# Forget attention of a four-layer block: scores as float32r products over all 128 rows, mask last

## Chip, cores and metric

The kernel runs on one core of one Trainium2 chip. The metric is the device time of one execution in microseconds (us). Three runs of the kernel before gave 1043.25, 1047.08 and 1048.91 us; their median is 1047.08.

## What is computed

The input is a sequence of 256 tokens of 1024 numbers. Two layers of a first block (a gated recurrence and a sparse attention), then an even layer, a feed-forward layer, an odd layer and another feed-forward layer run one after the other, all in float32. The change touches the odd layer alone, and in it the forget attention: eight heads of 64 numbers, causal, with a sum of log forget gates added to the logits.

```python
def forgetting_attention(q, k, v, f_logit, b_f):
    ...
    q, k, v = heads(q), heads(k), heads(v)
    log_f = jax.nn.log_sigmoid(f_logit.astype(jnp.float32) + b_f.astype(jnp.float32))
    c = jnp.cumsum(log_f, axis=1).transpose(0, 2, 1)
    ...
        logits = (jnp.einsum('bhqd,bhkd->bhqk', qb, k).astype(jnp.float32) * scale
                  + cb[..., None] - c[:, :, None, :])
        q_pos = start + jnp.arange(Q_BLOCK)
        logits = jnp.where(key_pos[None, :] <= q_pos[:, None], logits, -jnp.inf)
        p = jax.nn.softmax(logits, axis=-1)
        return jnp.einsum('bhqk,bhkd->bhqd', p.astype(v.dtype), v)
```

The term `cb` is the same for all keys of a query, so the softmax drops it.

## The kernel before

Every large product is made of float32r products in three parts: operands are split into a high part (rounded to float32r) and a low part (the rest, rounded too), and high x high, high x low and low x high are added up in PSUM (`mm3`, line 363). Weights come from HBM in pieces of 128x1024 numbers (512 KB): SP issues the load into `raw` (3 buffers), ScalarE writes the high part `whi`, VectorE the low part `wlo` (5 buffers each, `wload`, line 333). ScalarE and VectorE do this beside all their other work, in the order of one queue each, and so does SP with its loads. The order within each queue is set when the program is built, by a scheduler, and not by the order of the lines: products of a later step are put between those of an earlier one, where it expects a wait.

The odd layer (`odd_layer`, line 1139) projects v, the forget logits, q and k (`oq`, 8 groups of 24 products with 256 columns), then runs the attention in two halves of 128 queries (H = 0 with 128 keys, H = 1 with 256 keys), and beside it the projection of the gate `g` (`og`, 48 products of 512 columns, lines 1213 and 1214). Behind these come the gate's normalisation and mixing (`pm`, line 1224), the projection `u` (`ou`, line 1231), and the output projection.

q and k lie transposed, two heads in one group of 128 rows: head n has rows 0 to 63 if n is even and 64 to 127 if it is odd (`qT`, `kT`, lines 1178 to 1186, in float32). In `attention` (line 527) heads go by parity: for H = 0 four heads of one parity share a PSUM tile of 512 columns (`as`, two buffers), for H = 1 two heads. The tile begins with the mask for all 512 columns, a bf16 product with the identity. Then each head adds the forget sums (`extra`, line 1189: a float32r product of `cr`, which holds the sums in two parts, and `onehot`, which picks the head) and its q times k, in float32 over 64 rows:

```python
                mm(p3, identb, bm(causal[:, (1 - H) * P:], hb), True, False)
                for j in range(hb):
                    n = 2 * (j0 + j) + par
                    extra(p3[:, j, :], n, nk)
                    mm(p3[:, j, :], q(n), k(n)[:, :nk], False, j == hb - 1)
```

VectorE takes the maxima from PSUM (`anm`), ScalarE the exponentials with their sums (`pr`), VectorE scales them (`af`), TensorE transposes (`apt`), VectorE copies the transposes to SBUF (`pts`), and TensorE multiplies with v (`fo`).

Of the kernel before, what the change touches and what calls it, by code (L numbers as in the profile page):

```python
# [10 lines left out]
F32 = mybir.dt.float32  # L11
F32R = mybir.dt.float32r
BF = mybir.dt.bfloat16
U8 = mybir.dt.uint8
AF = mybir.ActivationFunctionType
OP = mybir.AluOpType
AX = mybir.AxisListType.X

P = 128
T = 256  # L20
# [200 lines left out]
def body(ctx: ExitStack, tc: tile.TileContext, a: dict, offs: dict, out: bass.AP):  # L221
# [4 lines left out]
    wk = ctx.enter_context(tc.tile_pool(name="wk", bufs=1))  # L226
# [5 lines left out]
    BUFS = dict(t2=2, lf=4, kT=3, vh=2, pr=2, pts=2, gate=4, s4=4, s1=2, w8=2, kk=1, y=2, nz=2,  # L232
                sm=4, sn=2, ss=4, sr=4, R=2, sh=3, sa=6, sc=6, sf=4,
                acc=3, pA=2, pM=1, pB=1, pC=1)
# [4 lines left out]
    def s2(name, dt=F32, tag="t2"):  # L239
        return wk.tile([P, 512], dt, tag=tag, name=name, bufs=BUFS[tag])  # L240

    def s4(name, dt=F32, tag="s4"):
        return wk.tile([P, 1024], dt, tag=tag, name=name, bufs=BUFS[tag])
# [10 lines left out]
    def dma(o, i):  # L254
        nc.sync.dma_start(o, i)
# [3 lines left out]
    def act(o, i, f, **kw):  # L259
        A.activation(o, i, f, **kw)  # L260

    def tt(o, x, y, op):
        V.tensor_tensor(o, x, y, op=op)  # L263
# [5 lines left out]
    def bm(ap, n):  # L269

        return ap.unsqueeze(1).to_broadcast([ap.shape[0], n, ap.shape[1]])
# [88 lines left out]
    def mm(o, l, r, start=True, stop=True):  # L360
        PE.matmul(o, l, r, start=start, stop=stop)  # L361
# [165 lines left out]
    def attention(H, q, k, pv, extra):  # L527

        nk = (H + 1) * P
        hb = 512 // nk
        sums = small("asum", 8, "sa")
        nm = small("anm", 8, "sa")
        for part in range(8 // (2 * hb)):
            pt2 = []
            for par in range(2):
                ps = ps_("as", "pA")
                p3 = ps.rearrange("p (h s) -> p h s", h=hb)
                j0 = part * hb  # L540
                mm(p3, identb, bm(causal[:, (1 - H) * P:], hb), True, False)
                for j in range(hb):
                    n = 2 * (j0 + j) + par
                    extra(p3[:, j, :], n, nk)
                    mm(p3[:, j, :], q(n), k(n)[:, :nk], False, j == hb - 1)
                c = slice(par * 4 + j0, par * 4 + j0 + hb)
                V.tensor_reduce(nm[:, c], p3, axis=AX, op=OP.max, negate=True)
                pr = s2("pr", tag="pr")
                pr3 = pr.rearrange("p (h s) -> p h s", h=hb)
                for j in range(hb):  # L550
                    i = par * 4 + j0 + j
                    act(pr3[:, j, :], p3[:, j, :], AF.Exp, bias=nm[:, i:i + 1], accum_out=sums[:, i:i + 1])
                f = small("af", 4, "sf")[:, :hb]
                V.reciprocal(f, sums[:, c])
                tt(pr3, pr3, bc(f, nk), OP.mult)
                pt = ps_("apt", ("pM", "pB")[par])
                for j in range(hb):
                    for b in range(H + 1):
                        i = b * hb + j
                        PE.transpose(pt[:, i * P:(i + 1) * P], pr3[:, j, b * P:(b + 1) * P], ident)  # L560
                pts = s2("pts", tag="pts")
                V.tensor_copy(pts, pt)
                pt2.append(pts)
            pv(j0, hb, pt2)
# [574 lines left out]
    def odd_layer(nx, nxt):  # L1139
# [35 lines left out]
        act(cr[:8], fe, AF.Copy)  # L1175
        tt(cr[32:40], fe, cr[:8], OP.subtract)

        qT = s4("oqT").rearrange("p (j t) -> p j t", j=4)
        kT = s4("okT").rearrange("p (j t) -> p j t", j=4)
        for nm, dst, sc in (("q", qT, 0.125), ("k", kT, 1.0)):  # L1180
            for j in range(0, 4, 2):
                ps = pacc("oq")
                for i in range(2):
                    proj_fm(ps[:, i * T:(i + 1) * T], x, win(f"{nm}{j + i}"))
                V.scalar_tensor_tensor(dst[:, j:j + 2, :], ps.rearrange("p (j t) -> p j t", j=2), sc, bm(R, 2),
                                       op0=OP.mult, op1=OP.mult)
        y = new_x("yE")

        def extra(s, n, nk):
# [2 lines left out]
        for H in range(2):  # L1192
            sl = slice(H * P, (H + 1) * P)
            po = ps_("fo", "pC")

            def pv(j0, hb, pts):
                for j in range(hb):
                    for b in range(H + 1):
                        for par in range(2):
                            n = 2 * (j0 + j) + par  # L1200
                            i = b * hb + j
                            mm(po[par * 64:(par + 1) * 64, (j0 + j) * P:(j0 + j + 1) * P], vs[b][:, n * 64:(n + 1) * 64],
                               pts[par][:, i * P:(i + 1) * P], b == 0, b == H)

            attention(H, lambda n: qT[(n % 2) * 64:(n % 2 + 1) * 64, n // 2, sl],
                      lambda n: kT[(n % 2) * 64:(n % 2 + 1) * 64, n // 2, :], pv, extra)
            split(y, slice(0, 4), sl, po.rearrange("p (j t) -> p j t", j=4))
        sb = s2("sgub", tag="y")
        sap = a["sgub"]
# [161 lines left out]
```

## Time and profile before

| | |
|---|---|
| median of three runs | 1047.08 us |
| the profiled execution | 1047.36 us, its span 1045.6 us |
| TensorE busy | 1020.2 us, 98% |
| its weight loads | 887.3 us, 85% |
| VectorE busy | 803.6 us, 77% |
| ScalarE busy | 593.5 us, 57% |
| GpSimd busy | 39.5 us, 4% |
| mean granted TensorE clock | 0.985 of full speed |
| HBM read | 164.36 MB, 158 GB/s over the span |

All times of rows count from the start of the span. PE is TensorE's products, PEld its weight loads, which run beside the products; DVE is VectorE, ACT ScalarE, POOL GpSimd, SP the engine that issues the loads. PEclk is the clock that was granted to TensorE, 1.00 being 2.4 GHz and 0.50 being 1.2 GHz. Products are pipelined and their ends are modelled, so the distance from one start to the next tells more than a duration.

### The profile page before, as it was taken

What the parts mean: (1) busy time and instruction counts of PE and PEld (TensorE: products, weight loads), DVE (VectorE), ACT (ScalarE), POOL (GpSimd) and SP (SyncE); (2) the same over time, 40 slices, a digit from 0 to 9 for tenths busy, and PEclk for the clock granted to TensorE, in tenths of its full rate; (3) what the DMA queues carried; (4) which work ended last, traced back from release to release, by engine and by line L of the source; (5) the groups of instructions that cost most, each with busy time, mean ns of one, the idle gap of its engine ahead of it and who ended that gap; (6) DMA issues with size and microseconds to landing.
All of it is one profiled execution on the core that took longest, in us unless ns stands there. A gap on an engine that the chain in (4) does not pass through costs nothing.

```text
span 1045.6 us, 17333 instructions
## 1 busy us (share of the span) xinstructions
PE 1020.2 (98%) x6604; PEld 887.3 (85%) x6604; DVE 803.6 (77%) x1508; ACT 593.5 (57%) x1049; POOL 39.5 (4%) x45
## 2 busy tenths in 40 slices
PE   7999999999999999999999999999999999999997
PEld 6778887778788776899889999998976889999996
DVE  5578888887788788778968877777644769777776
ACT  6654456567544564666657655556633557555553
POOL 1001100000002000000100000000000100000000
PEclk9999999999999999999999999999977999999999
DMA  8742643365523433655656666664631556666661
GB/s 300 242 145 55 217 130 90 93 222 157 185 69 108 137 101 92 184 161 174 208 160 188 198 186 193 184 183 132 213 109 51 165 147 201 186 188 192 184 182 60
DMA packets 47140, 166.54 MB, mean 159 GB/s; under 512 B 5456, under 2 KB 6480, under 8 KB 46416
## 3 DMA queue, kind: packets, MB, share of 16 engines
q1 hardware_dynamic: 47056, 165.43, 52.1%
q8 instruction: 52, 0.85, 0.3%
q14 instruction: 32, 0.26, 0.1%
HBM read 164.36 MB, written 1.05 MB: 158 GB/s over the span
## 4 chain that ended last, share of the span: by engine, by line
PE 78%; DVE 8%; ACT 5%; DMA 4%; issue 2%; POOL 2%; SPq 0%; POOLq 0%; ACTq 0%; DVEq 0%
PE up L361 24%; PE pd L361 11%; PE po L361 7%; PE as L361 3%; PE pg L361 3%; DVE wlo L263 3%; PE nz L361 2%; PE oq L361 2%; PE hgo L361 2%; DMA raw<-in_win_dram 2%; PE no L361 2%; PE pl L361 2%; POOL hr L408 2%; ACT whi L260 2%; PE Q L361 2%
## 5 line engine op out<-in xcount | busy, mean ns | idle before, releaser
L260 ACT ACTIVATE whi<-raw 128x1024 fp32r<-128x1024 f32 (+2 forms) x295 | 309.5, 1053 | 239.6 <-PE up L361 59.6
L263 DVE TENSOR_TENSOR wlo<-raw,whi 128x1024 fp32r<-128x1024 f32 (+2 forms) x295 | 357.1, 1213 | 93.5 <-ACT whi L260 90.8
L361 PE MATMUL pd<-whi,fhl 128*128 128x512 f32 x352 | 115.8, 391 | 0.0
L361 PE MATMUL up<-xFlo,whi 128*128 128x256 f32 x352 | 99.6, 283 | 0.5 <-DVE xFlo L432 0.5
L361 PE MATMUL up<-xDlo,whi 128*128 128x256 f32 x352 | 99.6, 283 | 0.5 <-DVE xDlo L432 0.5
L361 PE MATMUL up<-xDhi,whi 128*128 128x256 f32 x352 | 99.4, 283 | 0.2 <-ACT xDhi L260 0.2
L361 PE MATMUL up<-xFhi,whi 128*128 128x256 f32 x352 | 99.4, 283 | 0.2 <-ACT xFhi L260 0.2
L361 PE MATMUL up<-xFhi,wlo 128*128 128x256 f32 x352 | 99.5, 283 | 0.0
L361 PE MATMUL up<-xDhi,wlo 128*128 128x256 f32 x352 | 99.5, 283 | 0.0
L361 PEld LDWEIGHTS pd<-whi,fhl 128*128 128x128 f32 x352 | 66.2, 188 | 14.1 <-ACT fhl L260 0.9
L1027 DVE SCALAR_TENSOR_TENSOR fc<-fp,colp,fc 128x255 f32<-128x255 f32 (+1 forms) x176 | 73.5, 479 | 0.8 <-ACT fc L260 0.7
L361 PE MATMUL pd<-wlo,fhl 128*128 128x512 f32 x176 | 69.1, 392 | 0.0
L361 PEld LDWEIGHTS up<-xFlo,whi 128*128 128x128 f32 x352 | 67.5, 192 | 1.5 <-DVE xFlo L432 0.7
L361 PEld LDWEIGHTS up<-xDlo,whi 128*128 128x128 f32 x352 | 67.5, 192 | 1.5 <-DVE xDlo L432 0.7
L361 PEld LDWEIGHTS up<-xFhi,whi 128*128 128x128 f32 x352 | 67.3, 192 | 1.2 <-ACT xFhi L260 0.5
L361 PEld LDWEIGHTS up<-xDhi,whi 128*128 128x128 f32 x352 | 67.3, 192 | 1.2 <-ACT xDhi L260 0.5
L361 PEld LDWEIGHTS up<-xFhi,wlo 128*128 128x128 f32 x352 | 67.5, 192 | 0.0
L361 PEld LDWEIGHTS up<-xDhi,wlo 128*128 128x128 f32 x352 | 67.5, 192 | 0.0
L260 ACT ACTIVATE fc<-fp,colp 128x256 f32<-128x256 f32 x88 | 47.8, 589 | 2.7 <-DVE fp L263 2.6
L260 ACT ACTIVATE pr<-as,anm 128x128 f32<-128x128 f32 (+1 forms) x80 | 32.6, 423 | 27.9 <-PE apt L1011 9.6
L260 ACT ACTIVATE fhl<-fc 128x256 fp32r<-128x256 f32 x44 | 18.3, 415 | 44.9 <-DVE fc L263 44.9
L263 DVE TENSOR_TENSOR fp<-up,R 128x512 f32<-128x512 f32 x44 | 30.4, 691 | 15.8 <-PE up L361 15.8
(473 smaller groups left out, 2485.2 us busy)
## 6 DMA issues: line engine op xcount, KB each, us to landing
raw<-in_up_dram SPq DMA_DIRECT2D x88, 512.0 KB, 3.6
raw<-in_win_dram SPq DMA_DIRECT2D x64, 512.0 KB, 4.2
raw<-in_down_dram SPq DMA_DIRECT2D x44, 512.0 KB, 3.6
raw<-in_ein_dram SPq DMA_DIRECT2D x20, 512.0 KB, 4.1
raw<-in_oin_dram SPq DMA_DIRECT2D x20, 512.0 KB, 4.0
raw<-in_wout_dram SPq DMA_DIRECT2D x16, 512.0 KB, 3.6
raw<-in_wpg_dram SPq DMA_DIRECT2D x16, 512.0 KB, 4.2
cw<-in_cw_dram SPq DMA_DIRECT2D x4, 1024.0 KB, 5.3
```

What stands on the lines that cost most here:

```text
L260: A.activation(o, i, f, **kw)
L263: V.tensor_tensor(o, x, y, op=op)
L361: PE.matmul(o, l, r, start=start, stop=stop)
L408: G.tensor_tensor(o, v, mh[:, :v.shape[1]], op=OP.pow)
L1027: V.scalar_tensor_tensor(dst[:, k:], src[:, :T - k], w, dst[:, k:], op0=OP.mult, op1=OP.add)
```

## The change

The scores are made as three float32r products over all 128 rows. For each parity there is a tile of queries whose 64 own rows hold the high part and whose other 64 rows hold the low part of the same heads; the high part of the keys (`KA`) and their low part (`KB`) each stand twice, on both halves of the rows. So queries times `KA` is high x high plus low x high, and queries times `KB` is high x low plus low x low. ScalarE writes the high parts (8 copies of 64x512), VectorE the low parts (8 subtractions), and SP issues twelve copies of 64x512 from SBUF to SBUF that fill the other halves. The mask is the last product of a tile, and covers only the last 128 columns of each head.

```diff
@@ attention
-                mm(p3, identb, bm(causal[:, (1 - H) * P:], hb), True, False)
                 for j in range(hb):
                     n = 2 * (j0 + j) + par
+                    for i, kn in enumerate(k(n)):
+                        mm(p3[:, j, :], q(n), kn[:, :nk], j + i == 0, False)
                     extra(p3[:, j, :], n, nk)
-                    mm(p3[:, j, :], q(n), k(n)[:, :nk], False, j == hb - 1)
+                mm(p3[:, :, nk - P:], identb, bm(causal[:, P:], hb), False, True)
@@ odd_layer
-        qT = s4("oqT").rearrange("p (j t) -> p j t", j=4)
-        kT = s4("okT").rearrange("p (j t) -> p j t", j=4)
-        for nm, dst, sc in (("q", qT, 0.125), ("k", kT, 1.0)):
+        big = [wk.tile([P, 2, 4, T], F32R, tag="w8", name="oqk", bufs=BUFS["w8"]) for par in range(2)]
+        QA, KA = ([t[:, i] for t in big] for i in range(2))
+        KB = [wk.tile([P, 4, T], F32R, tag=n, name="okb", bufs=1) for n in ("kA", "kk")]
+        own = [slice(par * 64, (par + 1) * 64) for par in range(2)]
+        for nm, sc in (("q", 0.125), ("k", 1.0)):
             for j in range(0, 4, 2):
                 ps = pacc("oq")
                 for i in range(2):
                     proj_fm(ps[:, i * T:(i + 1) * T], x, win(f"{nm}{j + i}"))
-                V.scalar_tensor_tensor(dst[:, j:j + 2, :], ps.rearrange("p (j t) -> p j t", j=2), sc, bm(R, 2),
-                                       op0=OP.mult, op1=OP.mult)
+                t = s2("oqf", tag="t2").rearrange("p (j t) -> p j t", j=2)
+                V.scalar_tensor_tensor(t, ps.rearrange("p (j t) -> p j t", j=2), sc, bm(R, 2), op0=OP.mult, op1=OP.mult)
+                js = slice(j, j + 2)
+                lo = None if nm == "k" else s2("oql", F32R, "kT").rearrange("p (j t) -> p j t", j=2)
+                for par, o in enumerate(own):
+                    other = own[1 - par]
+                    hi = (QA if nm == "q" else KA)[par]
+                    act(hi[o, js], t[o], AF.Copy)
+                    if nm == "q":
+                        tt(lo[o], t[o], hi[o, js], OP.subtract)
+                        dma(hi[other, js].bitcast(F32), lo[o].bitcast(F32))
+                    else:
+                        tt(KB[par][o, js], t[o], hi[o, js], OP.subtract)
+                        for part in (hi, KB[par]):
+                            dma(part[other, js].bitcast(F32), part[o, js].bitcast(F32))
@@
-            attention(H, lambda n: qT[(n % 2) * 64:(n % 2 + 1) * 64, n // 2, sl],
-                      lambda n: kT[(n % 2) * 64:(n % 2 + 1) * 64, n // 2, :], pv, extra)
+            attention(H, lambda n: QA[n % 2][:, n // 2, sl], lambda n: [k[n % 2][:, n // 2] for k in (KA, KB)], pv, extra)
```

The scheduler puts the work of the stage in another order. On TensorE, at the end of the projection of k, the program before goes straight to the scores: `as_8216` is the tile of parity 0 and `as_8242` that of parity 1, each with its mask and four heads, and only two products of `og` stand ahead of the second half.

```order
L361 MATMUL oq_8149<-xEhi_7695,wlo_8183 128x256
L361 LDWEIGHTS identb_81
L361 MATMUL as_8216<-causal_80,identb_81 128x512
L361 MATMUL as_8216<-cr_7957,onehot_7786 128x128
L361 MATMUL as_8216<-okT_7962,oqT_7961 128x128
...
L361 MATMUL as_8242<-causal_80,identb_81 128x512
L361 MATMUL as_8242<-cr_7957,onehot_7786 128x128
L361 MATMUL as_8242<-okT_7962,oqT_7961 128x128
...
L361 MATMUL og0_8406<-whi_8384,xEhi_7695 128x512
L361 MATMUL og0_8406<-wlo_8385,xEhi_7695 128x512
```

Here no product of another step lies between the two tiles.

At the same place of the change `as_8252` is parity 0 and `as_8282` parity 1; `oqk_7961` and `oqk_7962` hold the queries and the high keys of the two parities, `okb_7963` and `okb_7964` the low keys.

```order
L361 MATMUL as_8252<-oqk_7961 128x128
L361 MATMUL as_8252<-okb_7963,oqk_7961 128x128
L361 MATMUL as_8252<-cr_7957,onehot_7786 128x128
...
L361 MATMUL as_8282<-okb_7964,oqk_7962 128x128
...
L361 MATMUL og0_8458<-whi_8436,xEhi_7695 128x512
...
L361 MATMUL as_8252<-oqk_7961 128x128 [waits DMAHW6_49,DMAHW5_49,Activation_49]
L361 MATMUL og1_8459<-whi_8436,xEhi_7695 128x512 [waits PE_49]
L361 MATMUL og1_8459<-wlo_8437,xEhi_7695 128x512
L361 MATMUL as_8252<-okb_7963,oqk_7961 128x128 [waits DMAHW7_49,DVE_49]
```

Two heads of each parity come first, then nine products of `og`, then the third head of parity 0, whose first product waits for the copy of the high keys and whose second, after three more products of `og`, waits for the copy of the low keys.

On SP, before, the last three loads of `u` (`raw_8533` to `raw_8601`) are followed by the load of `gfin`, which waits for TensorE. In the change the copies of the last two groups of keys stand between them, each behind its own wait, and `gfin` is loaded long before.

```order
L255 DMA raw_8585<-in_oin_dram 128x1024
L255 DMA raw_8623<-in_oin_dram 128x1024
L255 DMA oqk_7961<-oqk_7961 64x512
L255 DMA okb_7963<-okb_7963 64x512
L255 DMA oqk_7962<-oqk_7962 64x512
L255 DMA okb_7964<-okb_7964 64x512
L255 DMA raw_8653<-in_oin_dram 128x1024
L255 DMA raw_8693<-in_oout_dram 128x1024
```

The four copies are in the order in which their sources are written: high and low of parity 0, then of parity 1.

On ScalarE, before, the load of the table for the exponentials stands right behind the conversion `whi_8505`. In the change the two copies of the high keys and one more conversion (`whi_8587`, the second piece of `u`) come between.

```order
L260 ACTIVATE whi_8557<-raw_8555 128x1024 [waits DMAHW7_49,PE_49,Activation_49]
L260 ACTIVATE oqk_7961<-oqf_8237 64x512 [waits DVE_49]
L260 ACTIVATE oqk_7962<-oqf_8237 64x512
L260 ACTIVATE whi_8587<-raw_8585 128x1024 [waits DMAHW4_49,PE_49,Activation_49]
L260 ACT_TABLE_LOAD
L260 ACTIVATE pr_8267,asum_8250<-as_8252,anm_8251 128x128 [waits DVE_49]
```

The conversion `whi_8587` waits for TensorE, which has to be done with the buffer's old weights, those of the first twelve products of `og`.

## Rows read from the trace of the kernel before

**Rows 1.** The page, busy time, share of the span and instructions of each engine.
```profile
PE 1020.2 (98%) x6604; PEld 887.3 (85%) x6604; DVE 803.6 (77%) x1508; ACT 593.5 (57%) x1049; POOL 39.5 (4%) x45
```
**Rows 2.** Windows: length, busy PE, PEld, DVE, ACT, POOL, PEclk, DMA share, GB/s.
```profile
743.50:766.50 23.00, 23.00 (x194) 22.96 (x194) 13.68 (x16) 12.78 (x15) 0.31 (x1) 1.00 0.67 196
766.50:771.50 5.00, 5.00 (x26) 3.45 (x24) 2.61 (x3) 3.71 (x10) 0.00 (x0) 1.00 0.68 188
771.50:799.00 27.50, 27.50 (x87) 15.94 (x87) 11.34 (x22) 6.22 (x27) 0.00 (x0) 0.50 0.06 25
799.00:811.00 12.00, 12.00 (x66) 9.48 (x65) 5.75 (x6) 5.20 (x6) 0.00 (x0) 1.00 0.29 86
```
**Rows 3.** Timeline of PE, `og` and the first `ou`: start, length, operation.
```profile
805.35 0.39 PE L361 MATMUL og<-whi,xElo 128*128 128x512 f32 x1
805.58 0.39 PE L361 MATMUL og<-whi,xEhi 128*128 128x512 f32 x1
...
811.02 0.28 PE L361 MATMUL ou<-xEhi,whi 128*128 128x256 f32 x1
```
**Rows 4.** The tile `as`: instructions, min/median/max ns, first and last start, forms.
```profile
L361 PE MATMUL as<-okT,oqT x32: 272/605/792, 766.9 to 793.8; 64*128 64x128 f32 x16, 64*128 64x256 f32 x16
...
L361 PE MATMUL as<-cr,onehot x16: 326/486/775, 766.5 to 792.8; 128*128 128x128 f32 x8, 128*128 128x256 f32 x8
```
**Rows 5.** Timeline of PE, the first half's scores, at the full clock.
```profile
766.48 0.39 PE L361 MATMUL as<-causal,identb 128*128 128x512 bf16 x1
...
767.28 0.33 PE L361 MATMUL as<-cr,onehot 128*128 128x128 f32 x1
...
767.95 0.33 PE L361 MATMUL as<-cr,onehot 128*128 128x128 f32 x1
```
**Rows 6.** Timeline of PE, the second half's scores, at half the clock.
```profile
774.27 1.22 PE L361 MATMUL as<-okT,oqT 64*128 64x256 f32 x2
775.42 0.58 PE L361 MATMUL as<-cr,onehot 128*128 128x256 f32 x1
775.93 1.22 PE L361 MATMUL as<-okT,oqT 64*128 64x256 f32 x2
```
**Rows 7.** Timeline of PE, the projection of q, at the full clock.
```profile
744.40 0.28 PE L361 MATMUL oq<-xEhi,wlo 128*128 128x256 f32 x1
744.52 0.28 PE L361 MATMUL oq<-xEhi,whi 128*128 128x256 f32 x1
```
**Rows 8.** The tile `oq`: weight loads, min/median/max ns.
```profile
L361 PEld LDWEIGHTS oq<-xEhi,whi x64: 188/192/192, 743.3 to 766.0; 128*128 128x128 f32 x64
```
**Rows 9.** Lines, 766 to 811 us: count | busy us, mean ns | idle before, releaser.
```profile
L260 ACT ACTIVATE pr<-as,anm 128x128 f32<-128x128 f32 x8 | 2.8, 366 | 2.9 <-DVE anm L547 2.9
...
L547 DVE TENSOR_REDUCE anm<-as 128x4 f32<-128x512 f32 x2 | 1.4, 692 | 3.0 <-PE as L361 3.0
...
L260 ACT ACTIVATE yEhi<-fo 128x512 fp32r<-128x512 f32 x2 | 1.2, 600 | 5.7 <-PE fo L361 5.7
```
**Rows 10.** Timeline of ACT and DVE at the end of the projections.
```profile
766.56 1.06 ACT L260 ACTIVATE whi<-raw 128x1024 fp32r<-128x1024 f32 x1 [1.82 <-PE oq L361]
767.64 1.28 ACT L260 ACT_TABLE_LOAD   x1
...
766.68 0.69 DVE L1185 SCALAR_TENSOR_TENSOR okT<-oq,R 128x512 f32<-128x512 f32 x1 [0.68 <-PE oq L361]
767.65 1.22 DVE L263 TENSOR_TENSOR wlo<-raw,whi 128x1024 fp32r<-128x1024 f32 x1 [0.28 <-ACT whi L260]
```
**Rows 11.** DMA issues of the whole span: count, KB each, median us to landing.
```profile
sgub<-in_sgub_dram SPq DMA_DIRECT2D x2, 128.0 KB, 3.0
...
causraw<-in_c_causal_dram SPq DMA_DIRECT2D x1, 64.0 KB, 7.4
...
raw<-in_oin_dram SPq DMA_DIRECT2D x1, 32.0 KB, 1.7
```
**Rows 12.** Lines of the whole span, PE, the first layers' decay products.
```profile
L361 PE MATMUL D<-lev,lfh 128*128 128x512 f32 x32 | 13.9, 440 | 2.2 <-ACT lfh L260 2.2
```

## Prediction

> **What bounds the kernel now.** I read the page first: TensorE is recorded busy for 98% of the span [rows 1]. So the question is what it does in the stage that changes, and at which clock. The windows answer that [rows 2]. From the end of the projections of q and k (766.5 us) to the first product of `ou` (811.02 [rows 3]) lie 44.5 us, and TensorE is busy in all of them. The granted clock is 1.00 for the first 5 us, 0.50 for the next 27.5, 1.00 for the last 12: it falls from 2.4 to 1.2 GHz in the middle of the forget attention. In the slow stretch VectorE works 11.3 of 27.5 us, ScalarE 6.2, and DMA 6%: nothing but TensorE is near a bound there.
>
> Next, what one head's scores cost. A float32 product of q and k is issued as two passes (32 records for 16 products), the float32r product of `cr` and `onehot` as one [rows 4]. Read from start to start, a head of the first query half (128 keys) takes 767.95 - 767.28 = 0.67 us at the full clock [rows 5]; a head of the second half (256 keys) takes 775.93 - 774.27 = 1.66 us at half the clock [rows 6], so some 0.83 at the full one. Against this, the projections just before, all of them 128 rows in float32r, start one 256-column product every 0.12 us [rows 7]. Weights of 64 rows and of 128 rows alternate in the scores, and there a load doesn't hide under the product ahead.
>
> **The change, part by part, against the profiled execution** (1047.36 us, which the median of 1047.08 matches).
>
> *Scores.* Now three float32r products of 128 rows per head. No row shows 128-column products of this kind back to back. By columns they would cost half of 0.12; the upper end is a third of today's 0.67, 0.22. I take 0.12, since the same 192 ns weight load stands before each [rows 8], and a third of 0.67 holds the alternation that goes away. So a head costs 0.36, sixteen 5.8 us, where today it is 8 x 0.67 + 8 x 0.83 = 12.0: -6.2. The 24 narrow products put -1.4 to +2.4 on that.
>
> *Mask.* Six bf16 products of 512 columns at about 0.23 (the step of `og`, also 512 columns [rows 3]) become two of 512 and four of 256: -0.4.
>
> *Clock.* The stage is 44.5 us with 27.5 at half the clock; all at 2.4 GHz it would be 44.5 - 13.75 = 30.8. With the two savings 24.2 us of TensorE work are left, the 48 products of `og` among them.
>
> *High and low parts.* Eight ScalarE copies of 64x512 (0.60 each, as a 128x512 copy [rows 9]) and eight VectorE subtractions (0.69, as a 128x512 pass [rows 9]): 4.8 and 5.5 us. Six and six of them lie in the 23 us of the projections, where these engines work 12.8 and 13.7 us [rows 2] and TensorE sets the pace; the weights are converted five buffers ahead, and that covers them. Without this cover their 7.7 us would show. The last two and two cannot hide, next.
>
> *The last copies between halves.* This is the new wait. ScalarE's weight conversion ends at 767.62, VectorE's scaled keys at 767.37 and its weight residual at 768.87 [rows 10]. So the high keys of parity 0 are written at 768.2, of parity 1 at 768.8, their residuals at 769.6 and 770.3. Each is then copied by SP's queue onto the other 64 rows. The trace has no copy from SBUF to SBUF; a 128 KB load of 64 rows lands after 3.0 us, the extremes of small ones are 1.7 and 7.4 [rows 11]. I take 3.0, the same size and rows. The copies land at 771.3, 772.6, 773.0 and 773.4. TensorE has twelve products (1.4 us) and nine of `og` (2.1) from 766.5 on, until 770.0; waits 1.3 for the high keys; runs 0.8; waits 0.5 for the residual; parity 1 comes in time. Together 1.8 us; nothing at 1.7, 6.2 at 7.4. Eight other copies stand ahead of these in SP's queue, with weight loads behind them; those weights are due from 793 on, over 20 us later. The early load of `gfin` takes 512 KB out of SP's queue and costs nothing here.
>
> *Behind the wait.* ScalarE's next conversion waits for the twelfth `og` product (772.1) and stands ahead of the table load (1.28 [rows 10]) and the exponentials. Its VectorE partner ends at 774.4. Then come a maximum (0.69), four exponentials (0.37 each [rows 9]) for parity 0, to 776.6. TensorE's eight `og` products end at 776.2; the score buffer of the second half makes it wait 0.4. Further on the scaling of the probabilities, the copies of their transposes and the freed score buffers cost it some 0.1 to 0.3 each, about 1.3 us beyond today's. The last maxima and exponentials lie under the last twenty `og` products.
>
> *Sum.* 24.2 + 1.8 + 1.3 = 27.3 us instead of 44.5: -17.2. Behind the stage the gate's chain (its normalisation, then `pm`) finds `ou` to cover it as before; one `pm` comes some 0.5 us late. 1047.4 - 17.2 + 0.5 = 1030.7, **1031 us**. Four fifths of it is the clock.
>
> **A rule that speaks against it.** The projections' loads begin with the product ahead of them and last 192 ns, while products start every 0.12 us [rows 7, 8]: loads over all 128 rows do overlap. The Trainium skill, TensorE: Matmul & The Clock Gate (Part 3: Packing small matmuls — row/col tiling), says that a load overlaps running products only where its row group differs, which no two products of 128 rows do. The trace disagrees with that sentence; its price is among the rivals.
>
> **The rivals.**
>
> *The clock falls, but briefly* (chance 0.2). For it: the stretch from 770.0 to 773 has 1.8 us of waiting and short products, and the clock fell at 771.5 before. Against it: TensorE waited up to 2.2 us, for `lfh` in the first layer [rows 12], without falling, and dense `og` products now lie on both sides. It came back amid dense `og` work around 799. Low for 7 to 10 us, it costs half of that: 1034.5 to 1036.
>
> *It falls as before* (0.08). By 771.5 some 3.5 us of work are done, 20.7 left; 27.5 us at half the clock do 13.75 of it, 7 remain, and the waits hide in the slower work: the stage ends at 806, 5 us early, 1042.
>
> *Loads that do not overlap* (0.02). Then 48 products cost 0.19 + 0.12 = 0.31 instead of 0.12, +9: 1040.
>
> *The projections' cover fails* (0.03): a conversion of weights behind the new copies and subtractions comes late, and up to 7.7 us show: 1038.
>
> *Slower* (0.03). The place is the second high and residual copies in SP's queue. If they land after 7.4 us, the last at 777.8, TensorE stands idle for 6 us, the clock falls, and the rest of the scores, a chain of short steps, does not bring it back: some 20 us of work take 40, to 818 instead of 811, 1054. It decides only if both hold, late copies and a clock that stays low to the end of `og`; with the clock alone the stage ends near 814, 1050.
>
> **How the numbers follow.** The forecast, the clock held, has 0.64: 1028 to 1035 with the narrow products (-1.4 to +2.4) and the copies (-1.8 to +4.4). The range reaches from 1027 to 1040, over the brief fall, the failed cover and the missing overlap, and leaves the other two and some error of the sum outside. A measurement of this kernel tells about 0.5%, 5.2 us, from no change; faster means below 1041.8. All cases but the second and the slow ones lie there: 0.89; half of the second and the milder slow one are the same: 0.07; slower 0.04.
>
> **What would show it.** Right: clock 1.00 through the stage; a head's three products 0.36 apart; gaps of TensorE near 770 and 772 that end with copies landing at about 771.3 and 772.6; the first `ou` product near 794; behind it the old distances. Wrong: clock 0.50 in any of these windows; copies that land after over 4 us; a step of 0.2 us in the narrow products; or an `ou` that starts early while `po` does not.

## The result, and the profile after

The changed kernel takes **1034.12 us** (median of 4; 1032.62 to 1035.89), the kernel before beside it 1046.47 (median of 4): a ratio of 0.9884, 95% interval 0.9850 to 0.9919. Measured again on another chip it took 1034.02 against 1043.74, 0.9892 (0.9870 to 0.9914). It is faster, inside the range, 3 us above the forecast of 1031. The profiled execution is the slowest of the first four, 1035.89 us, with a span of 1034.1 (before: 1047.36 and 1045.6).

The busy line of the page, against [rows 1]: TensorE has lost 17 us of recorded work, VectorE and ScalarE have gained 4.4 and 3.4 us, the subtractions and copies of the high and low parts.

```profile
PE 1003.3 (97%) x6604; PEld 879.9 (85%) x6604; DVE 808.0 (78%) x1516; ACT 596.9 (58%) x1057; POOL 38.5 (4%) x45
```

Windows of the changed kernel, with the columns of [rows 2]: the projections, the gap behind them, the first half of the forget attention, the rest to the first product of `ou`, and the tail to just past the first of `po` (814.52).

```profile
745.30:768.27 22.97, 22.97 (x193) 22.93 (x192) 16.44 (x22) 16.34 (x21) 0.31 (x1) 1.00 0.71 204
768.27:771.30 3.03, 0.49 (x4) 0.24 (x2) 1.57 (x2) 0.97 (x2) 0.00 (x0) 1.00 0.99 248
771.30:780.40 9.10, 8.16 (x46) 6.38 (x46) 4.96 (x7) 5.14 (x14) 0.00 (x0) 1.00 0.77 224
780.40:798.28 17.88, 17.88 (x129) 14.08 (x129) 13.99 (x25) 9.73 (x29) 0.00 (x0) 1.00 0.22 72
798.28:814.60 16.32, 14.24 (x130) 13.55 (x130) 11.81 (x18) 7.50 (x11) 3.28 (x2) 1.00 0.36 104
```

Three things are to be seen. The granted clock stays at 1.00, where [rows 2] had 27.5 us at 0.50. The stage, 768.27 to 798.28, is 30.0 us long, where it was 44.5. And there is idle time that was not there: 2.5 us behind the projections with the DMA engines at a share of 0.99, 0.9 in the first half, 2.1 in the tail. The timeline of TensorE shows where:

```profile
768.15 0.28 PE L361 MATMUL oq<-xEhi,wlo 128*128 128x256 f32 x1
770.50 0.30 PE L361 MATMUL as<-oqk 128*128 128x128 f32 x1 [2.07 <-issue]
771.27 0.30 PE L361 MATMUL as<-okb,oqk 128*128 128x128 f32 x1 [0.47 <-DMA okb<-okb]
771.41 0.27 PE L361 MATMUL as<-cr,onehot 128*128 128x128 f32 x1
771.52 0.28 PE L361 MATMUL as<-oqk 128*128 128x128 f32 x1
...
776.88 0.30 PE L361 MATMUL as<-okb,oqk 128*128 128x128 f32 x1 [0.24 <-DMA okb<-okb]
...
780.39 0.38 PE L361 MATMUL as<-oqk 128*128 128x256 f32 x1 [0.70 <-ACT pr L260]
...
804.83 1.09 PE L361 MATMUL pm<-ws,og 128*64 128x128 f32 x16 [1.15 <-DVE og L263]
811.48 1.09 PE L361 MATMUL pm<-ws,og 128*64 128x128 f32 x16 [0.93 <-DVE og L263]
```

The narrow products start every 0.11 us, a head of three takes 0.33. But already the first score product comes 2.35 us behind the last product of `oq`; the view names no releaser for it, but the copy of its high keys landed just then, 4.6 us after its issue. The chain of waits that leads to the second product, the first that needs low keys, runs back through VectorE, ScalarE and SP's loads:

```profile
757.38 0.68 DVE oql L263
...
758.10 1.24 DVE wlo L263
...
759.35 4.73 DMA raw<-in_oin_dram
...
764.19 1.07 ACT whi L260
...
765.28 1.22 DVE wlo L263
766.50 0.61 DVE okb L263
...
767.13 4.01 DMA okb<-okb
```

VectorE's new subtraction `oql` (0.68) stands ahead of a weight residual `wlo`. That residual frees the buffer into which SP then loads the next piece of the gate's weights; the load lands after 4.73 us; ScalarE, which has waited 1.86 us for it by its timeline, converts it (`whi`) and only then, in the order of its queue, writes the high keys; then come the residual and the copy.

```profile
764.19 1.06 ACT L260 ACTIVATE whi<-raw 128x1024 fp32r<-128x1024 f32 x1 [1.86 <-DMA raw<-in_oin_dram]
```

Of the 11.5 us by which the span is shorter, the stage gives 14.5. Two things take back 3.2. Behind the stage, `pm` waits 2.1 us instead of 0.8: 1.4 more between the first products of `ou` and of `po`. Ahead of it, the projections of q and k end 1.8 us later, since in this execution the clock fell once in the first layer, where nothing was changed:

```profile
36.10:39.50 3.40, 3.40 (x18) 3.40 (x17) 2.17 (x3) 1.10 (x2) 0.00 (x0) 0.50 0.68 230
```

It fell behind the wait for `lfh` of [rows 12]. That wait is as long in both profiles, first before, then after, and before the clock stayed at 1.00 behind it:

```profile
35.24 0.74 PE L361 MATMUL D<-lev,lfh 128*128 128x512 f32 x2 [2.15 <-ACT lfh L260]
...
34.72 0.73 PE L361 MATMUL D<-lev,lfh 128*128 128x512 f32 x2 [2.16 <-ACT lfh L260]
```

### The profile page after: what moved, and what is told of

The parts are those of the page before. It is cut to its first block, busy times and chain, and to the rows that moved or that the text cites. A ratio compares the mean times of both kernels' runs of the same rounds, so it can differ in the third digit from the quotient of the medians.

```text
span 1034.1 us, 17375 instructions
## 1 busy us (share of the span) xinstructions
PE 1003.3 (97%) x6604; PEld 879.9 (85%) x6604; DVE 808.0 (78%) x1516; ACT 596.9 (58%) x1057; POOL 38.5 (4%) x45
## 3 DMA queue, kind: packets, MB, share of 16 engines
HBM read 164.36 MB, written 1.05 MB: 160 GB/s over the span
## 4 chain that ended last, share of the span: by engine, by line
PE 74%; DVE 9%; DMA 6%; ACT 5%; issue 2%; POOL 2%; SPq 0%; POOLq 0%; ACTq 0%; DVEq 0%
PE up L361 24%; PE pd L361 12%; PE po L361 7%; DVE wlo L263 3%; DMA raw<-in_win_dram 3%; PE pg L361 3%; PE nz L361 2%; PE as L361 2%; PE no L361 2%; ACT whi L260 2%; PE pl L361 2%; PE hgo L361 2%; POOL hr L408 2%; PE Q L361 2%; PE K L361 1%
```

## The experiments

Two questions: what holds the clock (the 64-row and 128-row products that no longer alternate, or something else), and what the copies between the halves cost and by which way. "Stage" is the stretch from the last product of `oq` to the first of `ou` in the profiled execution: 44.5 us before, 30.0 after. All ratios are to the kernel before on the same chip.

**1. The mask alone.** The kernel before, with the mask as the last product and as narrow as in the change:

```diff
-                mm(p3, identb, bm(causal[:, (1 - H) * P:], hb), True, False)
...
-                    extra(p3[:, j, :], n, nk)
-                    mm(p3[:, j, :], q(n), k(n)[:, :nk], False, j == hb - 1)
+                    extra(p3[:, j, :], n, nk, j == 0)
+                    mm(p3[:, j, :], q(n), k(n)[:, :nk], False, False)
+                mm(p3[:, :, nk - P:], identb, bm(causal[:, P:], hb), False, True)
```

> The kernel before with the mask alone changed (last product, 128 columns a head); scores stay 64-row float32 with a 128-row forget sum between them. Theory (it is the alternation of 64-row and 128-row weights in the scores that makes them slow and lets the clock fall): 0.4 us at most is saved, 0.50 of the clock stays in the middle of the forget attention, the stage from the last product of oq to the first of ou stays at 43 to 45 us, 1045 to 1047 us. Rival (the mask at the head of each tile is what opens the gap in which the clock falls): the clock stays at 1.00, the stage is some 30 us, 1031 to 1034 us.

Measured: 7 executions, 1032.86 to 1045.93, median 1035.48; ratio 0.9934 (0.9902 to 0.9967). Four of the seven lie at 1032.9 to 1035.5 with a mean clock of 0.996 to 0.998, two at 1041 (0.990 and 0.991), one at 1045.9 (0.985). The profiled one, 1032.86, kept the clock through the stage, by the window of it:

```profile
764.54:796.57 32.03, 32.03 (x177) 22.17 (x176) 19.30 (x31) 15.13 (x41) 0.00 (x0) 1.00 0.27 82
```

The starts of two neighbouring heads in each half, from its timeline of TensorE:

```profile
765.11 0.33 PE L361 MATMUL as<-cr,onehot 128*128 128x128 f32 x1
...
765.78 0.33 PE L361 MATMUL as<-cr,onehot 128*128 128x128 f32 x1
...
770.64 0.28 PE L361 MATMUL as<-cr,onehot 128*128 128x256 f32 x1
...
771.48 0.38 PE L361 MATMUL as<-cr,onehot 128*128 128x256 f32 x1
```

The expectation of the theory was wrong: with every alternation in place (a head still takes 0.67 us in the first half, 0.84 in the second, and 0.94 in the second where the mask follows) the clock can hold. It also gives a number the prediction could only estimate: the stage with the old scores at full clock is 32.0 us long, without any recorded idle time. The kernel before does the same now and then: of its 48 executions beside these experiments three took 1035.2, 1035.2 and 1035.8 us at a mean clock of 0.996, all others 1041.3 to 1049.3 at 0.991 or less; on the chip of this experiment it was two of 20. So the mask seems to shift the odds, on the evidence of seven executions.

**2. Forget sums of a tile first.** The same kernel, with the 128-row products of a tile ahead of its 64-row ones; float32 stays, no copies:

```diff
+                for j in range(hb):
+                    extra(p3[:, j, :], 2 * (j0 + j) + par, nk, j == 0)
                 for j in range(hb):
                     n = 2 * (j0 + j) + par
-                    extra(p3[:, j, :], n, nk, j == 0)
                     mm(p3[:, j, :], q(n), k(n)[:, :nk], False, False)
```

> The kernel before with its float32 products of 64 rows kept, but in each tile of scores all the forget sums of 128 rows first, then all the 64-row products, mask last: the row count changes twice a tile and no longer twice a head; no copies between halves. Theory (alternation): a head falls from 0.67 us to 0.4 or less at 128 keys, and the clock holds at 1.00; the stage is 28 to 32 us, 1029 to 1034 us. Rival (the two passes of a float32 product are slow in themselves, and the clock falls by them): a head stays at 0.6 us or more, the clock falls to 0.50 near 771, the stage stays above 40 us, 1043 to 1047 us.

Measured: 1031.90 us (1030.66 to 1032.23), ratio 0.9872 (0.9848 to 0.9895). The window of its stage:

```profile
765.27:794.28 29.01, 28.67 (x176) 21.50 (x175) 19.35 (x31) 15.13 (x41) 0.00 (x0) 1.00 0.29 92
```

A tile of four heads in its timeline of TensorE, sums, products and mask:

```profile
765.27 0.56 PE L361 MATMUL as<-cr,onehot 128*128 128x128 f32 x4
765.75 1.17 PE L361 MATMUL as<-okT,oqT 64*128 64x128 f32 x8
766.85 0.39 PE L361 MATMUL as<-causal,identb 128*128 128x512 bf16 x1
```

A head of 128 keys costs (766.85 - 765.27) / 4 = 0.40 us instead of 0.67: changing the row count less often saves 0.27 us a head, and float32's two passes take (766.85 - 765.75) / 8 = 0.14 each. (Here the number format changes with the row count; experiment 5 tells the two apart.) The whole gain of the change is reached by this order and the mask. It was measured once more beside the changed kernel:

> The kernel before with its 64-row float32 products, the sums of a tile first, mask last, no copies, beside the changed kernel on one chip. Theory (what the change gains is the end of the alternation and with it the clock; float32r and the copies add nothing beyond): as in its first measurement 1030.5 to 1032.5 us, 1 to 4 us below the changed kernel. Rival (its first measurement met only executions in which the clock happened to hold): medians of 1036 us and more, the clock at 0.50 near 771 in part of the executions.

Measured: 1033.31 (1031.03 to 1035.48), ratio 0.9890 (0.9868 to 0.9912), a little above the range expected; stage 29.0 again. In none of the nine executions of this kernel was the mean clock under 0.996. Beside it the changed kernel:

> The changed kernel once more, beside the next three on one chip. All theories: 1032.5 to 1036 us, the stage some 30 us with the clock at 1.00 and 2.5 to 3 us of waiting for the copies of the keys at the first heads; executions near 1035.7 are those in which the clock fell for a few us in some other place.

Measured: 1034.02 (1031.31 to 1036.00); stage 30.2 us, waits of 1.91 and 0.49 at the first heads. By the executions the two can't be told apart (0.9890 and 0.9892 with intervals of 0.004); by the profiles, from the end of `oq` to the first product of `po`, the regrouped kernel needs 43.9 us both times, the changed one 46.3 and 46.5.

**3. No copies.** The changed kernel with the twelve copies taken out and the halves that they filled zeroed once:

```diff
-                        dma(hi[other, js].bitcast(F32), lo[o].bitcast(F32))
...
-                        for part in (hi, KB[par]):
-                            dma(part[other, js].bitcast(F32), part[o, js].bitcast(F32))
```

> The changed kernel without the twelve copies between the halves (the other halves are zeroed once): it leaves out the product of the low parts of q with the high parts of k. All products keep their number and shape. Theory (the copies hold up SP's weight loads and then the first products, some 4 us of the stage's 30): the first score product starts within 1.5 us of the last product of oq, the third weight load of the gate comes 2 to 3 us earlier, the stage is 25.5 to 27 us, 1029 to 1031 us. Rival (behind the copies stands another wait, ScalarE's conversions and table load ahead of the first exponentials, so that the time comes back there): first products early, but idle TensorE before the second half's scores or the transposes grows by as much, 1032.5 to 1035 us.

Measured: 1033.78 (1031.49 to 1035.62), ratio 0.9890 (0.9870 to 0.9911). The stage of the profiled execution reaches from 766.48 to 795.20; the window in it where the clock was low:

```profile
770.20:773.50 3.30, 3.30 (x13) 2.93 (x13) 1.60 (x4) 1.71 (x9) 0.00 (x0) 0.50 0.44 144
```

The two waits of its scores, in the timeline of TensorE, and the conversion of the gate's weights ahead of its high keys, in that of ScalarE:

```profile
768.24 0.33 PE L361 MATMUL as<-oqk 128*128 128x128 f32 x1 [0.87 <-ACT oqk L260]
...
769.58 0.33 PE L361 MATMUL as<-okb,oqk 128*128 128x128 f32 x1 [0.45 <-DVE okb L263]
...
761.11 1.06 ACT L260 ACTIVATE whi<-raw 128x1024 fp32r<-128x1024 f32 x1 [0.89 <-DMA raw<-in_oin_dram]
```

Scores begin 0.12 us behind the last projection, and the stage takes 28.7 us although the clock fell for 3.3 of them; 27.1 without that fall, 2.9 under the changed kernel. The expected 1029 to 1031 us did not come: the mean clock was 0.995 to 0.997 in all six executions, against 0.996 to 0.999 of the changed kernel. So the copies cost about 3 us of the stage, but without them the executions gain nothing that can be measured; the profiled one shows that some of it goes to the clock. The time lies in the rival's range, but the rival's wait is not there: behind the first heads the scores wait for nothing. And the conversion still waits for its load, 0.89 us instead of 1.86, with no copy anywhere.

**4. Three float32r products of 64 rows, alternating.** No copies, no float32, the mask last: the scores of the kernel before with

```diff
+                    extra(p3[:, j, :], n, nk, j == 0)
+                    for qn, kn in qk(n):
+                        mm(p3[:, j, :], qn, kn[:, :nk], False, False)
...
+                o = slice((n % 2) * 64, (n % 2 + 1) * 64)
+                return [(big[0][o, a, n // 2, sl], big[1][o, b, n // 2, :]) for a, b in ((0, 0), (0, 1), (1, 0))]
```

> No copies: high and low parts stay on their own 64 rows, a head takes three float32r products of 64 rows (high by high, high by low, low by high) and, ahead of them, the forget sum of 128 rows: the alternation stays, float32 and the copies go. Theory (alternation costs about 0.1 us at each change of the row count, some 0.2 a head, and it decides the clock): a head of 128 keys takes 0.55 to 0.7 us, four products instead of three; either the clock falls as before, 1038 to 1043 us, or it holds, and 1030 to 1034 us come out since the wait for copies is gone. Rival (float32's two passes make the scores slow, alternation costs nothing): a head takes 4 x 0.11 = 0.45 us, the clock holds, 1028 to 1030 us.

Measured: 1048.55 (1043.59 to 1051.39), ratio 1.0046 (1.0017 to 1.0076): a little slower than the kernel before, and worse than either branch of the theory, though the first head of 128 keys takes 0.63 us, as it expects, and the second 0.73. A window of the stage:

```profile
772.40:799.80 27.40, 27.40 (x92) 19.27 (x93) 10.75 (x20) 7.25 (x32) 0.00 (x0) 0.51 0.00 1
```

The clock fell at 772.2 and came back at 799.5, the picture of [rows 2].

**5. The same, sums first.** The one order changed, as from 1 to 2.

> The kernel of the fourth experiment (three float32r products of 64 rows a head, no copies) with one thing changed: the forget sums of a tile stand ahead of its products, so that the row count changes twice a tile and not twice a head. Theory (alternation lengthens the steps and lets the clock fall): a head of 128 keys takes 0.45 to 0.5 us in the mean, the clock stays at 1.00, the stage is 27 to 30 us instead of 45, 1029.5 to 1033.5 us. Rival (products over 64 rows let the clock fall by themselves): 0.50 near 771 again, a stage over 38 us, 1040 us or more.

Measured: 1043.62 (1042.16 to 1045.49; 12 executions, mean clock 0.983 to 0.989), ratio 0.9993 (0.9973 to 1.0013). The rival was right: by the ratios grouping wins some 5 us on experiment 4 but doesn't save the clock, as the window from its fall to its return shows:

```profile
769.40:796.60 27.20, 27.20 (x101) 20.95 (x102) 11.34 (x21) 7.20 (x32) 0.00 (x0) 0.50 0.07 20
```

Ahead of the fall TensorE waited twice for the high and low parts, in its timeline:

```profile
767.99 0.32 PE L361 MATMUL as<-oqk 64*128 64x128 f32 x1 [0.39 <-ACT oqk L260]
...
769.33 1.33 PE L361 MATMUL as<-oqk 64*128 64x128 f32 x5 [0.65 <-DVE oqk L263]
```

Both kernels are float32r throughout, so they tell the row count from the number format. Sums, products and mask in the timeline of TensorE, at half the clock: a head of 256 keys with the sum ahead of it (experiment 4), and two heads with both sums first (this one):

```profile
777.76 0.58 PE L361 MATMUL as<-cr,onehot 128*128 128x256 f32 x1
779.21 0.40 PE L361 MATMUL as<-causal,identb 128*128 128x256 bf16 x1
...
775.32 0.78 PE L361 MATMUL as<-cr,onehot 128*128 128x256 f32 x2
777.60 0.40 PE L361 MATMUL as<-causal,identb 128*128 128x256 bf16 x1
```

That is 1.45 us against 2.28 / 2 = 1.14 a head, with the same products. So alternation sets the length of the scores (here and in experiment 2), but not by itself the fall of the clock. Why the clock falls here in all twelve executions, and in experiment 2's kernel in none of nine by their mean clocks, is not shown: the two differ in format, in the number of products and in these two waits.

**6. Copies from GpSimd's queue.** In the changed kernel:

```diff
-                        dma(hi[other, js].bitcast(F32), lo[o].bitcast(F32))
+                        nc.gpsimd.dma_start(hi[other, js].bitcast(F32), lo[o].bitcast(F32))
...
-                            dma(part[other, js].bitcast(F32), part[o, js].bitcast(F32))
+                            nc.gpsimd.dma_start(part[other, js].bitcast(F32), part[o, js].bitcast(F32))
```

> The changed kernel with its twelve copies issued from GpSimd's queue, which is idle there, instead of SP's; nothing else is moved. Theory (in SP's queue the copies of q wait for their subtractions and hold the weight loads behind them, so that ScalarE's conversion and the high keys come 1.5 us late): the gate's third weight load is issued 2 to 3 us earlier, the high keys are written at about 764 instead of 765.2, the wait at the first heads falls from 2.5 to 1.3 us or less, the stage is 28 to 29 us, 1031 to 1033 us. Rival (the transfer itself, 4 to 5 us beside the weight loads, is what counts, whoever issues it): copies land 4.5 us or more after their issue, the wait stays above 2 us, 1033 to 1036 us.

Measured: 1039.25 (1036.88 to 1041.67), ratio 0.9949 (0.9928 to 0.9969), 5 us slower than the changed kernel beside it and above both ranges. The theory's first half holds: high keys are written at 763.0 instead of 765.8. The rest went to the rival: the copies of the low keys land 5.6 to 6.5 us after issue, where in the changed kernel they took 2.2 to 4.0; the median, by the DMA issues of that kernel:

```profile
okb<-okb POOLq DMA_DIRECT2D x4, 128.0 KB, 6.2
```

TensorE waits twice, 3.8 us together, in its timeline:

```profile
768.50 0.30 PE L361 MATMUL as<-oqk 128*128 128x128 f32 x1 [1.40 <-DMA oqk<-oqk]
771.23 0.44 PE L361 MATMUL as<-okb,oqk 128*128 128x128 f32 x1 [2.44 <-DMA okb<-okb]
```

And then the clock falls, from 771.2 to 778.0; the window of that:

```profile
771.40:778.00 6.60, 6.60 (x22) 5.73 (x23) 0.00 (x0) 0.00 (x0) 0.10 (x1) 0.50 0.54 143
```

**7. Only the copies of q from GpSimd's queue.** The first of the two lines of experiment 6.

> The changed kernel with the four copies of the low parts of q issued from GpSimd's queue; the eight copies of the keys stay with SP. Theory (in SP's queue the copies of q hold up the weight loads): loads and the high keys come 2 us earlier, the key copies land 3 to 4 us after issue, the wait at the first heads falls from 2.5 us to 1 or less, 1031 to 1033 us. Rival (the DMA engines are full there, at a share of 0.9 to 1.0, so that what is won in the queue is lost in the transfer): the key copies land 5 us or more after issue, the wait stays at 2 us or more, 1033.5 to 1037 us.

Measured: 1035.23 (1032.13 to 1036.12), ratio 0.9917 (0.9887 to 0.9947). Both theories were half right. The waits at the first heads shrink to 0.93 and 0.43 us, the low keys land after 3.1. But the third head now waits 1.37 us (0.28 in the second profile of the changed kernel), and the second half's scores 1.18 (0.70 in its first profile, 1.18 in its second): the stage is 30.3 us, as before this edit. The chain to the third head:

```profile
762.84 5.91 DMA raw<-in_oin_dram
...
768.85 1.06 ACT whi L260
...
770.45 4.19 DMA oqk<-oqk
```

Again a long weight load, 5.91 us, ScalarE's conversion of it ahead of the high keys, and a copy of 4.19: for the stage the queue was not what counted. Nor is GpSimd's queue slower for every copy: those of q landed after 4.6 us in the median from it, against 5.6 from SP's in the changed kernel, so why the low keys of experiment 6 took so long is not shown. With the DMA engines at shares of 0.91 to 1.05 from 763 to 769 in this run and the last one, the wait only moved from the first heads to the third.

**8. No copies of q.** The changed kernel without the first of the two copies in experiment 3, its place zeroed once; those of the keys stay.

> The changed kernel without the four copies of the low parts of q, whose place is zeroed once: it leaves out the product of the low parts of q with the high parts of k. The eight copies of the keys stay. Theory of the queue: as the run with q on GpSimd's queue, within 0.7 us. Theory of the full DMA engines: with 512 KB less to move their share from 763 to 771 falls to 0.9 or below, the first key copies land 1 us or more sooner after issue than in that run, and the wait falls to 1.5 us or less while there it doesn't; 1031 to 1033 us.

Measured: 1034.09 (1031.90 to 1037.78), ratio 0.9913 (0.9881 to 0.9944); 1 us above the range expected, and not to be told from the changed kernel. In the profile the theory of the full DMA engines is borne out: the first scores start without a wait, the first copies of the low keys land within 2.8 us, one wait of 1.00 us for a copy is left at the third head, and 0.89 us for the exponentials ahead of the second half, the stage is 28.3 us, 1.7 shorter. The share did not fall to 0.9 in every window, as expected, but from 763 to 766 to 0.86, where the last run had 1.00.

**9. Sums first in the changed kernel.** The edit of experiment 2 on it.

> The changed kernel with the forget sums of a tile (128 rows, no copies needed) ahead of its products of q and k. Theory (the wait at the first heads is one for data alone): the eight sums of the first two tiles, 0.9 us, run before the copies land, the wait falls by 0.6 to 0.9 us, the stage is 29 to 29.5 us, 0.5 to 1 us less than the changed kernel beside it. Rival (TensorE is late there because its sums and the following order bind it, or the clock falls over the shorter products): no gain, or a fall of the clock and 2 to 10 us more.

Measured: 1032.67 (1030.47 to 1035.13), ratio 0.9885 (0.9863 to 0.9908); stage 28.5 us. The waits at the first heads fall from 2.5 to 1.15, with another 0.49 at the third:

```profile
768.25 0.30 PE L361 MATMUL as<-oqk 128*128 128x128 f32 x1 [0.54 <-issue]
769.15 0.30 PE L361 MATMUL as<-okb,oqk 128*128 128x128 f32 x1 [0.61 <-DMA okb<-okb]
```

So there it was a wait for data alone. The gain of 1.5 us in the profile is more than the 0.9 of the sums; its executions can't be told from those of the changed kernel.

**10. Both.** The edits of 7 and 9.

> Both edits on the changed kernel: copies of q from GpSimd's queue, and the forget sums of a tile first. Theory (queue): the wait at the first heads all but goes, the stage is 27.5 to 28.5 us, 1030 to 1032 us, under both kernels. Theory (full DMA engines): the sums win 0.9 us, the queue nothing; 1032.5 to 1035 us, no better than the sums first alone.

Measured: 1033.26 (1032.09 to 1034.47), ratio 0.9902 (0.9870 to 0.9934), in the range of the theory of the full DMA engines. The wait for the copies stands as one piece of 2.76 us at the third head, and the stage is 29.9 us: 0.3 less than in experiment 7, 1.4 more than with the sums first alone. So the queue doesn't help; what the sums add here is not clear.

No version is shown to beat the changed kernel or the regrouped one (experiment 2) by more than the executions scatter. The regrouped one is the simplest that reaches the time of the change.

## Why the prediction was right, point by point

*The clock, four fifths of the gain.* Right as an outcome: 1.00 through the stage, in both profiles of the changed kernel; the brief fall (0.2) didn't come, and came in experiments 3 and 6. Why it holds, the prediction did not work out, and the runs do not show it. Its argument against the brief fall, that the clock did not fall behind the wait for `lfh`, does not stand: that wait is 2.15 or 2.16 us long in all 14 profiles, and the clock fell behind it in 7 of them, both of the changed kernel among them. Nor did the clock before come back amid dense `og` work: ahead of 799 stand fourteen products of `fo` and two of `og`. The term was also mis-sized. I halved the 27.5 slow microseconds and had 30.8 us for the old stage at full clock; experiment 1 shows 32.0 plus the 0.4 of the mask, so the clock gives 44.5 - 32.4 = 12.1 us and not 13.75. Not every step halves: a head of the second half takes 0.84 or 0.94 us there at full clock, where half of the 1.66 of [rows 6] is 0.83; where the rest of the difference lies I have not traced. What I took for a property of the kernel before also varies from one execution to the next: three of 48 have the time and the mean clock of a stage without the fall, and of experiment 1, with the mask alone, four of seven.

*Scores.* Right, and a little better: 0.33 us a head of 128 keys, 0.36 of 256, against a forecast of 0.36. The narrow step is 0.11, within the bounds and close to the 0.12 that I took. The old scores at full clock, by experiment 1, are 0.67 and between 0.84 and 0.94, so that the saving is an estimated 7.0 us, not 6.2.

*A load behind the running product.* The step of 0.11 us with loads of some 190 ns, all over 128 rows, agrees with [rows 7, 8]. It speaks against the sentence of the Trainium skill (TensorE: Matmul & The Clock Gate, Part 3: Packing small matmuls — row/col tiling) that only loads of another row group overlap. What cost time was the change between 64 and 128 rows, 0.27 us a head in experiment 2.

*The last copies between halves.* The size came out near (3.5 us of recorded waits in the stage, 3.1 forecast), the place did not. The step that failed is "those weights are due from 793 on, over 20 us later". Their products are; their conversions are not, since ScalarE has them ahead of the high keys, and one of them waited 1.86 us for a load. I had the load of the weights as covered, but it starts only when VectorE's residual frees the buffer, VectorE has the new subtractions ahead of that, and the DMA engines are fuller: a share of 0.99 in the gap, where [rows 2] have 0.67 and 0.68. How much of the late load is the subtractions' and how much the copies' is not separated: without any copy the same conversion waited 0.89 us (experiment 3), and without those of q it did not wait for its load (experiment 8). So the first heads waited, 2.5 us, and the third, where I had put it, did not for parity 0 and 0.24 us for parity 1. The landing of 3.0 us, from [rows 11], holds for copies with little beside them; issues of the whole stretch, count, size, and median time to landing:

```profile
oqk<-oql SPq DMA_DIRECT2D x4, 128.0 KB, 5.6
oqk<-oqk SPq DMA_DIRECT2D x4, 128.0 KB, 3.4
okb<-okb SPq DMA_DIRECT2D x4, 128.0 KB, 3.0
```

The four early ones of the low parts of q take 5.6 us, the first low key on the chain above 4.01. One of the signs that I had named for being wrong, "copies that land after over 4 us", was there.

*The rival of the projections' cover* (0.03) was nearer to the truth than its chance: a conversion did come late behind new copies and subtractions, only not one that the projections waited for.

*Behind the wait and behind the stage.* The second half's scores waited 0.70 us against 0.4, and 1.18 in the second profile of the changed kernel; `pm` came 1.4 us late in two waits, not 0.5 in one.

*The sum.* Forecast 27.3 us for the stage, measured 30.0: +1.65 from the clock's term, -0.8 from the scores, +0.4 of recorded waits, and some 1.5 that no single row shows. Of these, 0.65 can be worked out: a product ahead of a gap is recorded to its end, 0.28 us, where the next one could have started 0.12 after it, at each of four gaps. The rest stays open. With 1.8 us ahead of the stage and 0.9 more behind it than forecast, 1030.7 becomes 1036.1; the profiled execution took 1035.9. Two other executions, at 1032.6 with a mean clock of 0.998 and 0.999, have no traces; that they lack the fall in the first layer is likely, and not shown. The regrouped kernel shows what it can cost: its two profiles, without and with that fall, have spans of 1028.8 and 1031.4 us.

*What stays open* is why the clock falls. Idle time doesn't decide it alone: it held through waits of 2.07 and 0.47 us in the changed kernel and 2.76 in experiment 10, and fell behind 0.87 and 0.45 in experiment 3 and behind none in [rows 2]. The wait for `lfh` in the first layer, the same work and the same 2.2 us every time, had either outcome. Nor do alternation (experiments 1 and 5) or 64-row products (experiment 2) decide it. What the profiles show is how long it stayed low once it had fallen: about 27 us over 64-row scores (before, experiments 4 and 5), 3.3 and 6.6 us over 128-row ones (experiments 3 and 6). Executions of the kernel before with mean clocks of 0.988 to 0.991, where the profiled one has 0.985, have no traces; an estimate from that figure is that they were low for less time. The 45 executions of all kernels with 128-row scores have mean clocks of 0.993 or more, the nine of experiment 2's kernel 0.996 or more; the kernel before reached that in 3 of 48.

## What to carry to other kernels

Group products by the number of rows their weights fill before rewriting them: an order that changed 64 and 128 rows twice a tile instead of twice a head, in float32, gave as much here as float32r, doubled keys and twelve copies. With three float32r products of 64 rows it shortened the scores as well, but the clock fell and the time was that of the kernel before. When a step takes a new input over DMA, follow the engines' queues back from its source: a load that is due late for its own product can stand, through an in-order conversion, ahead of a copy that is due at once. And where the clock of a stage can go either way, time many executions and read the mean clock of each, before one profile is taken for the kernel.

## What the runs showed that was not expected

The times of the kernel before fall into two groups, 1035 and 1041 to 1049 us, with mean clocks of 0.996 and at most 0.991, and moving and narrowing the mask, worth 0.4 us of TensorE work, came with a shift of the odds from 3 in 48 to 4 in 7, a small number. Three float32r products of 64 rows let the clock fall in the profile in either order; with two float32 passes of the same rows, grouped, the mean clock stayed at 0.996 or more in nine executions. One wait of 2.2 us in the first layer, with the same work around it, was followed by a fall of the clock in 7 profiles of 14. A 128 KB copy between halves landed after 2.2 us at the least and 5.7 at the most from SP's queue in the changed kernel, and the copies of the low keys after 5.6 to 6.5 us from GpSimd's.
